# Loading half of x already transposed, and running two products of blocks two and three between the token halves of block one

## Chip, core and metric

The kernel runs on one core of one Trainium2 chip. The metric is the device time of one execution in microseconds (us). The engines are named as in the profile: PE is TensorE's matmul side and PEld its weight load, DVE is VectorE, ACT is ScalarE, POOL is GpSimd, SP is SyncE. SP issues nearly all transfers, in order.

## What is computed

One layer of an encoder trunk, cut to what matters here:

```python
h = rms_norm(x, norm_w)                       # x is 1024 tokens x 2048 columns, float32
proj = h @ w_in                               # 2048 x 6656: 13 column blocks of 512
y = concat(retention(rq, rk, rv) * silu(rg), window_attention(aq, ak, av) * silu(ag))
out = rms_norm(x + y @ w_out, final_norm_w)
```

The change touches only the start of `h @ w_in`. The norm weight `nw` belongs to a column of x and the factor `rms` to a token. Since `rms` multiplies whole tokens, the kernel may put it on the result of the projection instead of on x.

## The kernel before

**Products.** A float32 operand is split into a high part in the type float32r and the remainder, also float32r. A product of two split operands is three matmuls (`mm3`, lines 99, 100, 101: high times high, high times remainder, remainder times high). One matmul has a 128x128 weight and 512 columns. ACT makes the high part of a weight operand (`operand`, line 194), DVE the remainder (`low`, line 85). The weight operands have two buffers (`AHEAD`), so the next one can only be written when the product before last is done.

**Blocks.** The projection is worked off in column blocks of 512, each in two halves of the depth (`PHASES`). The first phase takes five blocks (`akv`, `aq0`, `aq1`, `rk0`, `rq0`) with the first 1024 columns of x; below they are blocks one to five. Blocks two and later use Winograd's form of Strassen's scheme: seven products instead of eight (numbers 1, 2, 6, 5, 7, 3, 4), whose operands are sums of quarters of w (`a11`, `a12`, `a21`, `a22`, made by DVE with `add`, line 92, and `sub`, line 95) and sums of quarters of x (tiles `c1` to `c7`, split on ACT, line 88, and DVE, line 85). Block one needs no sums of x, so it is computed plainly, with eight products.

**Steps.** A product is four steps of six matmuls; `advance()` counts a step, and generators (`start`, `tick`, `idle`) hang work on the count. Block one takes 32 steps, every later block 28. The order of PE, SP and POOL is as written. For the first 33 steps the order of DVE and ACT is as written as well (`all_manual`); after that a scheduler in the build places their instructions, moving them ahead of others where it sees a gap, except those that `behind()` pins.

**The opening.** x arrives with tokens on the partitions. Four 128x128 transposes on PE turn one column group of one token half into a bank `ax` (lines 1017, 1037 and 470), and ACT and DVE read it. For tokens 0 to 511 they write the high part (line 999), the remainder (line 1003) and a copy (lines 1009, 1011), all unscaled by `rms`. For tokens 512 to 1023 the rows are scaled by `rms` first, then turned. The sums of squares (`squares`, ACT line 448, DVE line 450) give `rms`; transposed into a row over tokens (`rows`), it scales the first half's copy (line 1089). The unscaled results of block one and of product 1+2 of block two go to memory, are loaded again later, multiplied by `rows` and stored again (lines 1102 to 1109). Matmuls of the identity with itself (line 1147) run on PE until the first data are there.

**After the sums.** Once the tiles of x are made, `keep` writes them to memory, and `second_part` loads the other 1024 columns of x transposed (`x_t`), scales them (line 509) and forms the sums for the second depth half, while blocks four and five run. A quarter of w is loaded by `quarter` (line 201) into the one buffer of its kind, as soon as the operand made from the old one is finished. The results leave the banks `pj` through ACT copies (`evict`, line 328) and DVE adds (line 92) into eight buffers `ct`, from which SP stores them (line 290).

Of the kernel before, what the change touches and what calls it, by code (L numbers as in the profile page):

```python
# [18 lines left out]
P = 128  # L19
SQ = 32  # L20
S = 1024
# [37 lines left out]
def hybrid_layer_kernel(  # L59
    ctx: ExitStack,  # L60
    tc: tile.TileContext,
    x, x_t, w_in, w_out, norm_w, decay_fwd, decay_bwd, gn_w, gn_b, sink, final_norm_w,
# [106 lines left out]
    rows_d = dram.tile([1, HALF], F32, name="rows_d")  # L169
# [37 lines left out]

    def operands():

        for u in range(len(units)):  # L210
            a = dict(w_next)
            if u == 0:

                for (n, k), last in zip(QUARTERS + QUARTERS[:2], (False, False, True, True, True, True)):
                    if (n, k) == (1, 1):
                        if not last:
                            left = wp.tile([P, M, 2 * P], F32R, name="s2", tag="s2")
                        op = wp.tile([P, M, 2 * P], F32R, name="wH", tag="wH", bufs=AHEAD), left
                        if last:
                            nc.scalar.copy(out=op[0], in_=a[n, k])  # L220
                        else:
                            split(*(t[:, 0:2] for t in op), a[n, k][:, 0:2])
                    else:
                        op = operand(a[n, k])
                    if last:
                        w_next[n, k] = quarter(*units[1], n, k)
                    yield op
                continue

            def then(n, k):  # L230
                if u + 1 < len(units):
                    w_next[n, k] = quarter(*units[u + 1], n, k)
                else:
                    place_free(n, k)

# [59 lines left out]
    def evict_second(b, i, a, bank, held):  # L295

        def store(n, m, t):
            stores.append((True, pr[BLOCKS[b] // P + 2 * n + a][:, half(m)], t))

        if i == 1:  # L300
            held["u", a] = t = ct()
            nc.scalar.copy(out=t, in_=bank)
            held[1, a] = ct()
            nc.vector.tensor_tensor(out=held[1, a], in0=t, in1=rows_of[0], op=ALU.mult)
        elif i in (6, 5):
            held[i, a] = ct()
            add(held[i, a], bank, held[1, a])
        else:
            t = held.pop(({2: "u", 7: 5, 3: 6, 4: 1}[i], a))
            add(t, bank, t)  # L310
            store(*{2: (0, 0), 7: (1, 1), 3: (0, 1), 4: (1, 0)}[i], t)
            if i == 2:
                unscaled.append(stores[-1][1])
# [25 lines left out]
    unscaled, rows_of = [], []  # L339

# [4 lines left out]
    def first_block(b, of):  # L345


        ops_, t = {}, 0
        for m, order in ((0, QUARTERS), (1, QUARTERS[2:] + QUARTERS[:2])):
            for n, k in order:  # L350
                if k == 1:
                    banks = [pj(), pj()]
                if t not in (0, 3, 4):
                    prepare()
                if t not in (4, 5):
                    ops_[n, k] = ready.popleft()
                wH, wL = ops_[n, k]
                for q in range(M):
                    if q == M - 1:
                        flush()  # L360
                    for a in range(2):
                        cH, cL = of[k, m]
                        if t == 0 and q < 2:
# [5 lines left out]
                            for po, w in left:  # L369
                                nc.tensor.matmul(po, w, cL[:, q], start=False, stop=False)  # L370
# [1239 lines left out]
```

## Time and profile before

| | us |
|---|---|
| median of 3 runs (lowest to highest) | 1515.04 (1514.44 to 1516.33) |
| the profiled execution: its own time | 1510.86 |
| the profiled execution: its span | 1508.7 |
| PE busy in the span | 1487.5 |
| DVE busy in the span | 1116.5 |
| ACT busy in the span | 681.2 |

The span is the time from the first to the last instruction; the execution's own time is 2.2 us longer. Mean durations of an instruction include a stretch in which the next one already runs, so work is best costed from the distance between starts. A group's row ends with the idle time before it and what ended that. In the table of windows a row gives for each engine the busy time and the count, then the granted clock, the share of the DMA engines and GB/s.

### The profile page before, as it was taken

Reading aid. Unit: us, or ns where it says so; the run is one execution under the profiler, and the core shown is the slowest. Engines: PE = TensorE matmul, PEld = TensorE weight load, DVE = VectorE, ACT = ScalarE, POOL = GpSimd, SP = SyncE. Lnnn points to the kernel's source line nnn. Section 1 sums busy time; section 2 is a strip of 40 time slices with the busy share of each in tenths; the row PEclk is TensorE's granted clock in tenths of the full one; section 3 lists DMA queues with packets and bytes.
Section 4 is the critical chain, followed back from the end, with each engine's and each line's share of the span. In section 5 each row is a group of like instructions: output and inputs, shape, how many; then the busy total and the mean of one; then the engine's idle time right before and its main releaser. Section 6 shows DMA issues by size and latency. Waiting matters only on the chain.

```text
span 1508.7 us, 20071 instructions
## 1 busy us (share of the span) xinstructions
PE 1487.5 (99%) x7154; PEld 1250.8 (83%) x7154; DVE 1116.5 (74%) x1928; ACT 681.2 (45%) x1108; POOL 150.9 (10%) x177
## 2 busy tenths in 40 slices
PE   9999999999999999999999999999999999999997
PEld 8878788888888888888888788887888888888886
DVE  6898694557768576767988789887656966776766
ACT  7533363334545454533444444444444664542425
POOL 0000001111010000011221100001211102020001
PEclk9999999999999999999999999999999999999999
DMA  8278748889584636798867665589887899495656
GB/s 329 63 281 346 286 168 215 226 202 259 143 265 154 196 133 199 287 311 196 175 160 170 161 193 170 183 290 335 218 235 190 180 211 207 96 207 169 213 178 254
DMA packets 140997, 318.88 MB, mean 211 GB/s; under 512 B 31425, under 2 KB 53345, under 8 KB 131554
## 3 DMA queue, kind: packets, MB, share of 16 engines
q1 hardware_dynamic: 116850, 266.74, 53.0%
q0 software_dynamic: 19728, 36.71, 16.5%
q10 hardware_dynamic: 4320, 14.17, 2.8%
q8 instruction: 56, 0.92, 0.3%
q14 instruction: 43, 0.35, 0.1%
HBM read 197.23 MB, written 128.71 MB: 216 GB/s over the span
## 4 chain that ended last, share of the span: by engine, by line
PE 83%; DVE 5%; issue 5%; DMA 4%; POOL 1%; ACT 1%; SPq 0%; POOLq 0%; ACTq 0%; DVEq 0%
PE pj L101 21%; PE pj L99 21%; PE pj L100 21%; PE ax L100 5%; PE ax L101 5%; PE ax L99 5%; PE ax L874 2%; DVE wL L85 2%; PE ax L656 1%; DMA pr<-ct 1%; DMA g<-mix 1%; PE ax L844 1%; PE ax L925 1%; POOL pr L292 1%; DMA ct<-pr 1%
## 5 line engine op out<-in xcount | busy, mean ns | idle before, releaser
L99 PE MATMUL pj<-c,wH 128*128 128x512 f32 x1444 | 573.1, 397 | 2.6 <-ACT wH L194 2.6
L101 PE MATMUL pj<-c,wL 128*128 128x512 f32 x1440 | 563.9, 392 | 6.6 <-DVE wL L85 6.5
L100 PE MATMUL pj<-c,wH 128*128 128x512 f32 x1444 | 563.6, 390 | 0.0
L101 PEld LDWEIGHTS pj<-c,wL 128*128 128x128 f32 x1440 | 270.8, 188 | 68.2 <-DVE wL L85 11.0
L99 PEld LDWEIGHTS pj<-c,wH 128*128 128x128 f32 x1444 | 271.9, 188 | 54.7 <-ACT wH L194 3.8
L100 PEld LDWEIGHTS pj<-c,wH 128*128 128x128 f32 x1444 | 272.0, 188 | 51.5 <-DVE c L1003 0.2
L85 DVE TENSOR_TENSOR wL<-a,wH 128x1024 fp32r<-128x1024 f32 x157 | 191.2, 1218 | 103.1 <-ACT wH L194 54.3
L194 ACT CAST wH<-a 128x1024 fp32r<-128x1024 f32 x129 | 135.5, 1050 | 176.7 <-PE pj L100 142.3
L328 ACT COPY ct<-pj 128x512 f32<-128x512 f32 x192 | 111.2, 585 | 209.3 <-PE pj L101 192.6
L92 DVE TENSOR_TENSOR ct<-pj,ct 128x512 f32<-128x512 f32 x164 | 108.7, 684 | 39.8 <-PE pj L101 39.4
L292 POOL DMA_DIRECT2D pr<-ct x88 | 78.0, 960 | 527.8 <-DVE ct L92 433.7
L85 DVE TENSOR_TENSOR wL<-s,wH 128x1024 fp32r<-128x1024 f32 x56 | 68.3, 1221 | 57.9 <-ACT wH L194 50.7
L100 PE MATMUL pj<-wL,c 128*128 128x512 f32 x224 | 87.2, 389 | 0.6 <-DVE wL L85 0.6
L99 PE MATMUL pj<-wH,c 128*128 128x512 f32 x224 | 87.1, 389 | 0.0
L101 PE MATMUL pj<-wH,c 128*128 128x512 f32 x224 | 87.1, 389 | 0.0
L100 PE MATMUL ax<-wL,c 128*128 128x512 f32 x208 | 81.2, 390 | 0.0
L99 PE MATMUL ax<-wH,c 128*128 128x512 f32 x208 | 80.9, 389 | 0.0
L101 PE MATMUL ax<-wH,c 128*128 128x512 f32 x208 | 80.9, 389 | 0.0
L88 ACT CAST wH<-a 128x1024 fp32r<-128x1024 f32 (+1 forms) x30 | 30.7, 1023 | 61.9 <-PE pj L101 35.0
L194 ACT CAST wH<-s 128x1024 fp32r<-128x1024 f32 x50 | 52.5, 1051 | 6.9 <-DVE s L95 6.9
L646 ACT ACTIVATE s<-s,nm 128x385 f32<-128x385 f32 (+1 forms) x64 | 37.6, 589 | 28.5 <-DVE nm L641 26.2
L100 PEld LDWEIGHTS pj<-wL,c 128*128 128x128 f32 x224 | 42.0, 188 | 9.8 <-DVE wL L85 1.0
(242 smaller groups left out, 2063.9 us busy)
## 6 DMA issues: line engine op xcount, KB each, us to landing
a<-in_w_in_dram SPq DMA_DIRECT2D x103, 512.0 KB, 5.3
kept<-c SPq DMA_DIRECT2D x28, 1024.0 KB, 7.7
c<-kept SPq DMA_DIRECT2D x28, 1024.0 KB, 7.4
pr<-ct SPq DMA_DIRECT2D x94, 256.0 KB, 5.5
pr<-ct POOLq DMA_DIRECT2D x88, 256.0 KB, 5.7
a<-in_w_out_dram SPq DMA_DIRECT2D x18, 512.0 KB, 4.5
rx<-pr SPq DMA_DIRECT2D x64, 128.0 KB, 5.7
ysrc<-pr ACTq DMA_DIRECT2D x16, 512.0 KB, 6.5
```

Of the source, the lines that this page charges most:

```text
L85: return nc.vector.tensor_tensor(out=dst, in0=src, in1=high.bitcast(F32), op=ALU.subtract)
L88: behind(pinned, nc.scalar.copy(out=dst_h, in_=src))
L92: nc.vector.tensor_tensor(out=dst, in0=a, in1=b, op=ALU.add)
L99: nc.tensor.matmul(po, aH, bH, start=first, stop=False, **kw)
L100: nc.tensor.matmul(po, aH, bL, start=False, stop=False, **kw)
L101: nc.tensor.matmul(po, aL, bH, start=False, stop=last, **kw)
L194: behind(pinned, nc.scalar.copy(out=wH, in_=src))
L292: nc.gpsimd.dma_start(out=dst, in_=t, accum_op=ALU.add)
L328: nc.scalar.copy(out=t, in_=bank)
L646: nc.scalar.activation(out=s[:, 0:w + 1], in_=s[:, 0:w + 1], func=AF.Exp, scale=-1.0, bias=nm, accum_out=den)
L656: nc.tensor.transpose(pt[:, blk(j)], s[:, blk(j)], ident)
L874: nc.tensor.matmul(p, k_tok[:, c // 2, :, c % 2], vd[:, c, d], start=True, stop=True)
```

## The change

**x transposed.** The first 1024 columns of x come a second time as input `x_f`, with columns on the partitions, cut into column half and token half; they are loaded straight into `src0`. The 64 transposes of x are gone, and with them the copies out of the banks. x with tokens on the partitions is still loaded, for the sums of squares alone. The norm weight and two other vectors come as one small input `vecs`.

**Order of PE.** Block one's first token half (16 steps) is followed by products 1 and 2 of blocks two and three (`early`, 8 steps each, unscaled, on the unscaled first token half), then by block one's second half (16 steps), then by the other five products of blocks two and three in the order 5, 6, 3, 7, 4 (`rest`). So the step at which block three ends, 88, is the same as before.

**Scaling.** DVE multiplies each column group by `nw` and `rows` at once (`scale`, line 1087). Product 1 of blocks two and three waits in its banks and is scaled into `ct` (line 414); the sum of products 1 and 2 is stored unscaled (8 tiles instead of 6) and rescaled later from `rows` directly (line 1228).

**Written order.** A table `plan` gives the work of ACT and DVE by step; their order is as written up to step 66 instead of 33. `second_part` starts at step 76 instead of 62.

The core of the diff:

```diff
+    def mixed(a, then):
+        a11, a12, a21, a22 = (a[q] for q in QUARTERS)
+        s2 = wp.tile([P, M, 2 * P], F32, name="s2", tag="s2")
+        sub(a11, a11, a21)
+        yield
+        add(a21, a21, a22)
+        yield
+        op = [wp.tile([P, M, 2 * P], F32R, name=n, tag=n, bufs=AHEAD) for n in ("wH", "wL")]
+        nc.scalar.copy(out=op[0], in_=a21)
+        yield
+        sub(s2, a22, a11)
+        yield
+        low(op[1], a21, op[0])
+        then(2, 1)
+        yield op
...
-            behind(clock[0] >= 33, sub(a11, a11, a21))
+            behind(True, sub(a11, a11, a21))
             sub(s2, a22, a11)
             yield op
-            yield operand(s2, clock[0] >= 33)
+            yield operand(s2, True)
...
+    def rest(b):
+        if b not in held_of:
+            first_scaled(b)
+        held = held_of[b]
+        Y, X = [pj(), pj()], [pj(), pj()]
+        for i in (5, 6, 3, 7, 4):
+            if b != units[1][1] or i == 4:
+                prepare()
+            bank = X if i in ON_X else Y
+            products(i, bank, ready.popleft(), comb[i], i in (5, 6), True, lambda a: evict_rest(b, i, a, bank[a], held))
...
+                if p == 0 and b in blocks[:3]:
+                    if b == blocks[0]:
+                        plain(b, 0, quarters, first_ops)
+                        for e in blocks[1:3]:
+                            early(e)
+                        plain(b, 1, quarters, first_ops)
+                    else:
+                        rest(b)
...
-        if clock[0] == 33:
+        if clock[0] == 66:
             all_manual.close()
...
+    load_first(0, 0, 0, 1)
+    nc.scalar.dma_start(out=vec_t, in_=vecs)
+    half_of_a11(0)
+    load_first(0, 0, 1, 1)
+    half_of_a11(2)
+    load_first(0, 0, 2, 2)
+    a12 = quarter(*u0, 1, 2)
+    load_first(1, 0, 0, 2)
+    load_first(1, 0, 2, 2)
+    a21 = quarter(*u0, 2, 1)
+    a22 = quarter(*u0, 2, 2)
...
+    idling = pj()
+    for _ in range(18):
+        nc.tensor.matmul(idling[:, 0:P], ident, ident, start=True, stop=True)
...
+    w_next[1, 1] = quarter(*u1, 1, 1)
+    load_row(4)
+    load_row(5)
+    w_next[1, 2] = quarter(*u1, 1, 2)
+    load_row(6)
+    load_row(7)
+    early_quarter(1)
+    load_row(0)
+    load_row(1)
+
+    def load_rest():
+        load_natural(6, 2, 3)
+        load_row(2)
+        early_quarter(2)
+        load_row(3)
+        load_first(0, 1)
...
+    at(22, square, 3, 0, True)
+    at(22, square, 3, 1, False)
+    at(23, factors_of, 0, 4)
+    at(24, lambda: ready.append(operand(early_w[2])))
...
+    at(76, lambda: start(second_part()))
```

Three places show the moved instructions. The first is the start of ACT's program, with the waits of each row. `vec_t` holds the norm weight, `c1` the split x, `a11` a quarter of w, `xt` and `src` are x before and after it is turned. Before:

```order
L526 DMA vec_189<-in_norm_w_dram 16x128
L436 DMA xt_183<-in_x_dram 128x2x256 x2
L1155 ACT_TABLE_LOAD
L1155 COPY vec_t_169<-pj_228 128x16 [waits PE_49]
L88 CAST wH_247<-a11_192 128x512 [waits DMAHW3_49]
L999 ACTIVATE c1_220<-ax_215,vec_t_169 128x512 [waits DVE_49,PE_49]
```

Now:

```order
L992 DMA vec_t_168<-in_vecs_dram 128x32
L989 DMA a11_190<-in_w_in_dram 128x512 x2
L1012 ACT_TABLE_LOAD [waits DMAHW1_49,DMAHW0_49]
L1012 ACTIVATE c1_207<-src_181,vec_t_168 128x512 [waits DVE_49]
L1012 ACTIVATE c1_207<-src_181,vec_t_168 128x512 [waits DMAHW3_49]
```

The table load had no wait; now it stands behind two transfers (the first piece of x and `vecs`).

The second place is DVE from the last operand of block two (`wL`, product 4) on. `wL` is the remainder of a weight operand, `ct` results, `a11`, `a21`, `s2` the sums of w, `c1`, `c2`, `c4` tiles of x. Before, down to the second operand of block three:

```order
L85 TENSOR_TENSOR wL_890<-a22_390,wH_889 128x1024
L85 TENSOR_TENSOR c1_220<-src_182,c1_220 128x1024 x2
L92 TENSOR_TENSOR ct_801<-pj_686,ct_801 128x512
L92 TENSOR_TENSOR ct_806<-pj_687,ct_806 128x512
L85 TENSOR_TENSOR wL_929<-a11_816,wH_928 128x1024
L85 TENSOR_TENSOR c2_221<-src_182,c2_221 128x1024 x2
L92 TENSOR_TENSOR ct_727<-pj_684,ct_727 128x512
L92 TENSOR_TENSOR ct_734<-pj_685,ct_734 128x512
L85 TENSOR_TENSOR wL_969<-a12_818,wH_968 128x1024
```

Now, down to the first operand that block three still needs (product 5):

```order
L85 TENSOR_TENSOR wL_866<-a22_373,wH_865 128x1024
L414 TENSOR_TENSOR ct_946<-ax_506,rows_270 128x512
L85 TENSOR_TENSOR c4_853<-tt_688,c4_853 128x1024
L92 TENSOR_TENSOR ct_779<-pj_750,ct_779 128x512
L92 TENSOR_TENSOR ct_784<-pj_751,ct_784 128x512
L95 TENSOR_TENSOR a11_829<-a11_829,a21_697 128x1024
L85 TENSOR_TENSOR c2_208<-src_181,c2_208 128x1024
L92 TENSOR_TENSOR a21_697<-a21_697,a22_869 128x1024
L95 TENSOR_TENSOR s2_902<-a22_869,a11_829 128x1024
L85 TENSOR_TENSOR c2_208<-src_181,c2_208 128x1024
L85 TENSOR_TENSOR wL_906<-a21_697,wH_905 128x1024
```

Block three used to begin with quarters of w as they are loaded; now its next product needs a sum, and nine instructions stand between the two operands where four stood.

The third place is DVE in block four, up to the operand of product 6 (`wL<-s2`). `src` is the second depth half of x, scaled in place by line 509 (now 537), `tt` its sums. Before:

```order
L85 TENSOR_TENSOR wL_1211<-a11_1090,wH_1210 128x1024
L509 SCALAR_TENSOR_TENSOR src_982<-src_982,vec_t_169,rows_522 128x1024 x2
L95 TENSOR_TENSOR tt_1339<-src_982 128x1024
L85 TENSOR_TENSOR wL_1252<-a12_1092,wH_1251 128x1024
L95 TENSOR_TENSOR a11_1090<-a11_1090,a21_1052 128x1024
L95 TENSOR_TENSOR tt_1340<-src_982,tt_1339 128x1024
L95 TENSOR_TENSOR s2_1255<-a22_1172,a11_1090 128x1024
L1108 TENSOR_TENSOR ct_1189<-ct_1189,ct_1187 128x512
L1108 TENSOR_TENSOR ct_1190<-ct_1190,ct_1187 128x512
L92 TENSOR_TENSOR a21_1052<-a21_1052,a22_1172 128x1024
L95 TENSOR_TENSOR tt_1388<-src_982 128x1024
L85 TENSOR_TENSOR wL_1296<-s2_1255,wH_1295 128x1024
```

Now (the operands of products 1 and 2 stand further up, with two more scalings, a sum and two adds behind the first of them):

```order
L95 TENSOR_TENSOR s2_1154<-a22_1072,a11_1038 128x1024
L537 SCALAR_TENSOR_TENSOR src_1032<-src_1032,vec_t_168,rows_270 128x1024
L92 TENSOR_TENSOR a21_910<-a21_910,a22_1072 128x1024
L537 SCALAR_TENSOR_TENSOR src_1032<-src_1032,vec_t_168,rows_270 128x1024
L95 TENSOR_TENSOR tt_1340<-src_1032,tt_1339 128x1024
L95 TENSOR_TENSOR tt_1386<-src_1032 128x1024
L537 SCALAR_TENSOR_TENSOR src_1032<-src_1032,vec_t_168,rows_270 128x1024 x2
L95 TENSOR_TENSOR src_1032<-src_1032 128x2x512
L95 TENSOR_TENSOR tt_1387<-src_1032,tt_1386 128x1024
L92 TENSOR_TENSOR ct_1182<-pj_1148,ct_1182 128x512
L92 TENSOR_TENSOR ct_1187<-pj_1149,ct_1187 128x512
L85 TENSOR_TENSOR wL_1191<-s2_1154,wH_1190 128x1024
```

Between the finished sum `s2` and the operand made from it there stood 4 instructions; now there are 11, eight of them scalings and sums of the second depth half.

More of the change, by code (lines that the diff above doesn't have):

```diff
@@ L293, in flush, with evict_rest @@
         stores.clear()
[L295 to L305, printed above, removed]
+    def evict_rest(b, i, a, bank, held):
+        if i in (5, 6):
             held[i, a] = ct()
@@ L502, in second_part @@
                 yield from idle(3)
-        rows = rows_of[1]
-        yield from rows_from(rms[:, 4:8], rows[:, half(1)])
         yield
@@ L1068, in rows_from @@
[L1068 to L1099 removed]
+    quarters, first_ops = {}, {}
@@ new lines, in hybrid_layer_kernel @@
+    load_row(5)
[11 more added lines that the diff above has]
+        load_first(0, 1)
+        for n in (2, 1), (2, 2):
+            w_next[n] = quarter(*u1, *n)
+        load_first(1, 1)
+    both = st.tile([P, S], F32, name="rows")
+    rows_of.extend((both[:, half(0)], both))
+    factors = {}
@@ new lines, in spread, with turn_rows, scale @@
+    def spread(m):
+        t = factors[m] = st.tile([P, HALF], F32, name="factors")
+        nc.vector.tensor_copy(out=chunks(t), in_=rms[:, 4 * m:4 * m + 4].rearrange("p (t o) -> p t o", o=1).broadcast_to([P, 4, P]))
+    def turn_rows(m, pt):
+        for t in range(4):
+            nc.tensor.transpose(pt[:, blk(t)], factors[m][:, blk(t)], ident)
+        nc.scalar.copy(out=both[:, half(m)], in_=pt)
+    def scale(s, k, m):
+        t, i = src0[:, s, k, half(m)], s * M + k
+        nc.vector.scalar_tensor_tensor(out=t, in0=t, scalar=nw[:, i:i + 1], in1=both[:, half(m)], op0=ALU.mult, op1=ALU.mult)
@@ new lines, in hybrid_layer_kernel, with step, at @@
+    mixed_first = mixed(w_next, then_of(1))
+    def step(n=1):
+        for _ in range(n):
+            if (op := next(mixed_first)) is not None:
+                ready.append(op)
+    plan = {}
+    def at(n, what, *args):
+        plan.setdefault(n, []).append((what, args))
+    at(6, lambda: ready.append(operand(w_next[1, 1])))
+    at(8, square, 4, 0, True)
+    at(8, square, 4, 1, True)
+    at(10, square, 5, 0, True)
+    at(10, square, 5, 1, False)
+    at(11, lambda: ready.append(operand(w_next[1, 2])))
@@ L1100, in scale_first, with opening, rescaled @@
+    at(76, lambda: start(second_part()))
+    at(112, lambda: start(decays()))
+    def opening():
+        for n in range(max(plan) + 1):
+            for what, args in plan.get(n, ()):
+                what(*args)
+            yield
+    def rescaled():
+        yield from idle(74)
         for i in range(0, len(unscaled), 2):
-            r = ct()
-            nc.sync.dma_start(out=r, in_=rows_d.to_broadcast([P, HALF]))
             es = [ct() for _ in range(2)]
```

501 lines of the change are left out of this document (237 added, 264 removed).

## The prediction

> **What bounds the kernel now.** I read the page's busy times first, then the windows of the opening, the waits of PE, and the timeline of DVE where PE waits. The page:
>
> ```profile
> span 1508.7 us, 20071 instructions
> PE 1487.5 (99%) x7154; PEld 1250.8 (83%) x7154; DVE 1116.5 (74%) x1928; ACT 681.2 (45%) x1108; POOL 150.9 (10%) x177
> ```
>
> PE is idle for 21 us of the whole span. So a change gains by taking work off PE or by closing a wait of PE, and nothing else. The change ends with block four; behind it the order hangs on PE's steps, so that a time won or lost there is carried to the end. The opening in windows (last column GB/s):
>
> ```profile
> 5.00:10.00 5.00, 4.78 (x27) 4.28 (x26) 2.31 (x4) 2.06 (x4) 0.00 (x0) 1.00 1.05 377
> 10.00:15.00 5.00, 5.00 (x32) 4.30 (x31) 3.72 (x6) 4.09 (x7) 0.00 (x0) 1.00 1.03 419
> 15.00:20.00 5.00, 5.00 (x28) 4.04 (x27) 4.82 (x7) 4.79 (x8) 0.00 (x0) 1.00 1.02 419
> 20.00:25.00 5.00, 5.00 (x23) 4.00 (x22) 4.67 (x9) 4.83 (x9) 1.24 (x1) 1.00 0.97 397
> 60.00:80.00 20.00, 19.64 (x87) 15.93 (x86) 19.90 (x21) 9.94 (x12) 0.00 (x0) 1.00 0.26 79
> 80.00:100.00 20.00, 19.29 (x85) 15.37 (x83) 20.00 (x22) 10.28 (x11) 0.00 (x0) 1.00 0.64 217
> ```
>
> Up to 25 us the DMA engines are full, and between 60 and 100 us DVE is: 39.9 of 40 us. There PE already waits for DVE's remainders of weight operands (first 160 us; columns: total, times, longest):
>
> ```profile
> PE pj L101 <- DVE wL L85: 1.1, 2, 0.7
> ```
>
> So this stage has two limits that lie close together, PE and DVE. DVE's pace there, back to back:
>
> ```profile
> 62.13 1.22 DVE L85 TENSOR_TENSOR wL<-a,wH 128x1024 fp32r<-128x1024 f32 x1
> 63.27 1.22 DVE L95 TENSOR_TENSOR a<-a,a 128x1024 f32<-128x1024 f32 x1
> ...
> 67.81 1.28 DVE L304 TENSOR_TENSOR ct<-ct,rows 128x512 f32<-128x512 f32 x2
> 69.02 1.22 DVE L92 TENSOR_TENSOR a<-a,a 128x1024 f32<-128x1024 f32 x1
> ...
> 124.95 2.48 DVE L509 SCALAR_TENSOR_TENSOR src<-src,vec_t,rows 128x1024 f32<-128x1024 f32 x2
> 127.34 1.28 DVE L92 TENSOR_TENSOR ct<-pj,ct 128x512 f32<-128x512 f32 x2
> ```
>
> From start to start, 1024 elements cost 1.14 us, 512 cost 0.60 (two in 1.21), and the two-factor scaling costs 1.195 (two in 2.39). For 512 elements I estimate that scaling at 0.66: the fall from 1.14 to 0.60 taken from 1.195. PE's pace shows where ACT waits for products:
>
> ```profile
> 127.19 1.06 ACT L194 CAST wH<-a 128x1024 fp32r<-128x1024 f32 x1 [3.66 <-PE pj L100]
> 132.62 1.05 ACT L194 CAST wH<-a 128x1024 fp32r<-128x1024 f32 x1 [4.38 <-PE pj L100]
> ```
>
> A product is 5.43 us, a step 1.3575. ACT's cast can only start when the product that used its buffer ends, so these two are the ends of the fifth and the sixth of block three's seven products, and block three ends at 132.62 + 5.43 = 138.05.
>
> **The start: nothing.**
>
> ```profile
> 1.36 2.93 PE L1147 MATMUL pj<-ident 128*128 128x128 f32 x12 [1.36 <-POOL ident masks.py:199]
> ...
> 2.25 1.28 ACT L1155 ACT_TABLE_LOAD   x1 [2.25 <-issue]
> ...
> 5.27 0.62 ACT L88 CAST wH<-a 128x512 fp32r<-128x512 f32 x1 [0.56 <-DMA a<-in_w_in_dram]
> ...
> 7.57 0.61 PE L1147 MATMUL pj<-ident 128*128 128x128 f32 x4
> ...
> 8.40 0.50 PE L366 MATMUL pj<-c,wH 128*128 128x512 f32 x1 [0.22 <-ACT c L999]
> ```
>
> The first real matmul starts at 8.40. Six identity matmuls are 12 records of 0.244 us; the last two are four records of 0.15. The 18 of the changed kernel are 36 records without a gap: they end at 1.36 + 8.8 = 10.2 if all go at the first pace and at 1.36 + 2.93 + 24 x 0.15 = 7.9 if all but 12 go at the last. I take 8.5. ACT's chain is behind that cover: the table load now waits for the first piece of x and the vector, about 5.3 by the piece of w that landed at 5.27, plus 1.28 for the load and about 0.6 for a pass over 512 columns: 7.2.
>
> **The transposes: -6.2 us of PE.** Of the 64, eight lie before 8.40. The other 56 stand between matmuls; in the chain that ended last each group of four costs
>
> ```profile
> 12.32 0.44 PE ax L1037 x4
> ```
>
> so 14 x 0.44 = 6.2. The two groups that turn the rows stay. Counted from 8.5, 88 steps and 0.9 for those two end at 128.9, against 138.05: 9.2 less, 6.2 of it transposes and the rest the waits and slips of the old opening. This is what PE would gain if nothing made it wait.
>
> **Input and the start of DVE's long stretch: 43.8 us.** Now x comes twice.
>
> ```profile
> 25.55 1.06 ACT L448 ACTIVATE junk<-xt 128x1024 bf16<-128x1024 f32 x1 [0.40 <-DMA xt<-in_x_dram]
> ```
>
> Here ACT waits for the last row tile of the old first list, 8.4 MB behind the start (2.1 of x, four quarters of 0.52, four rows of 1.05). In the new list SP queues 14.7 MB up to row tile 3, the last that the first token half's `rms` needs: 2.1 of x, eight quarters of w and eight row tiles. The 6.3 MB more take 15.0 us at 419 GB/s, so it lands at about 40.5. On ACT follow a square (1.06), two bank copies and the cast of block three's second operand.
>
> ```profile
> L194 ACT CAST wH<-a 128x1024 fp32r<-128x1024 f32 x129 | 135.5, 1050 | 176.7 <-PE pj L100 142.3
> L328 ACT COPY ct<-pj 128x512 f32<-128x512 f32 x192 | 111.2, 585 | 209.3 <-PE pj L101 192.6
> ```
>
> That is 1.06 + 2 x 0.585 + 1.05 = 3.3, so DVE gets to that operand's remainder at 43.8. PE needs it at step 28, 8.5 + 38.0 + 0.4 = 46.9: in time. The Trainium skill ("DMA: Bandwidth & Descriptors", Bandwidth) puts what HBM gives one core at about 358 GB/s; by it the 6.3 MB take 17.6 us and everything below comes 2.6 later. The windows show 397 to 419, so the measurement decides.
>
> **Blocks two and three: PE waits 6 us.** From 43.8 on DVE always has the next instruction ready. Up to the last operand of block two (`wL_866`) the order has 27 of 1024 elements, 16 scalings, 19 of 512 and a spread of the factors, which no quoted row shows and which I put at 0.4, below an operation of 512: 30.8 + 10.6 + 11.4 + 0.4 = 53.2. I add 1.4 for two places where DVE must wait, once for ACT's cast of a sum made one instruction earlier (1.05) and once for a product. It ends at 98.3. PE without waits begins that product (step 64) at 96.3 and needs the remainder 0.45 later, behind two matmuls of 0.226: 1.5 us of wait. Up to `wL_906`, the operand of block three's first remaining product, come 7 more of 1024 and 3 of 512, 9.8 us: 108.2. In there the quarter `a22` also has to land; its buffer is free at 98.3, and
>
> ```profile
> a<-in_w_in_dram SPq DMA_DIRECT2D x103, 512.0 KB, 5.3
> ```
>
> makes it 103.6, just as DVE reaches its sum. PE would need `wL_906` at 96.3 + 1.5 + 5.43 + 0.45 = 103.7: another 4.5 us. From there 26.7 us of matmuls lead to the end of block three at 134.9, 3.1 us before 138.05. So of the 9.2, 6.0 are waited away. The cause is the order: product 5 comes first and needs a sum of two quarters, one of which is loaded only when the block before is finished with the old one.
>
> **Block four: PE waits 6.7 us more.** I count from the end of block three's last product but one, 134.9 - 5.43 = 129.5. DVE adds its results (1.2), makes the operand of block four's product 1 (1.1) and then, up to `wL_1191`, has 10 of 1024, 6 scalings of 1.195 and 4 of 512: 11.4 + 7.2 + 2.4 = 21.0. With 0.1 of handing over it is 152.9. PE needs it after product 4, eight steps and 0.45: 134.9 + 11.3 = 146.2. The same sum for the old kernel, from the adds on, is 15.0 (9 of 1024, 2 scalings, 4 of 512), and the trace confirms it:
>
> ```profile
> 133.26 1.28 DVE L92 TENSOR_TENSOR ct<-pj,ct 128x512 f32<-128x512 f32 x2
> ...
> 147.18 1.22 DVE L85 TENSOR_TENSOR wL<-s,wH 128x1024 fp32r<-128x1024 f32 x1
> 148.31 1.22 DVE L95 TENSOR_TENSOR tt<-src,tt 128x1024 f32<-128x1024 f32 x1
> ```
>
> 133.26 to 148.3 is 15.0, and PE's need was at 138.05 + 11.3 = 149.35, one us later. So the old kernel had no wait here. The new one is at 152.9: 3.6 us behind it.
>
> **Behind that: zero, -1 to +2.4.** In the old block four DVE, in order, stood 5.7 us in front of a rescaling whose load was late, and operands behind it were late:
>
> ```profile
> 162.42 1.29 DVE L1108 TENSOR_TENSOR ct<-ct 128x512 f32<-128x512 f32 x2 [5.73 <-DMA ct<-pr]
> 165.36 1.22 DVE L85 TENSOR_TENSOR wL<-s,wH 128x1024 fp32r<-128x1024 f32 x1 [1.64 <-ACT wH L194]
> ```
>
> SP had issued that load at 153.21, 9.2 us ahead:
>
> ```profile
> 153.21 2.76 SPq L1105 DMA_DIRECT2D ct<-pr  x2
> ```
>
> The operand was due at 138.05 + 27.15 + 0.45 = 165.65; its high part came at 165.36 and its remainder at 166.5, which with the third matmul pushed back cost about 1. In the new order SP stands, ahead of the load, in front of a quarter of w whose buffer is free only when product 7's operand is made: product 6 ends at 157.9, then a copy, a cast and a remainder, 160.7. With the load 1 us behind that and 5.3 to 9.2 us long, a rescaling (0.6) and the remainder (1.1), product 3's operand is there at 168.7 to 172.6; it is due at 152.9 + 16.3 = 169.2. So the wait is 0 to 3.4 where about 1 was. I take no difference. Small vectors, `decays` without its transpose and the dropped broadcast load run beside full PE and count nothing; uncovered they are under 0.5.
>
> **Sum.** -9.2 + 6.0 + 6.7 = +3.5; from the two instants, 152.9 - 149.35 = +3.6. The profiled execution took 1510.86, so 1514.5; on the median of 1515.04 it is 1518.6. A measurement of this kernel can tell about 0.2%, 3 us, from no change.
>
> **Rivals.**
> - *DVE keeps up (faster).* All 9.2 remain and the time is 1505.8. It decides at `wL_906`: PE without waits needs it at 96.3 + 5.43 + 0.45 = 102.2, so DVE's 64.4 us from 43.8 on would have to be 6.0 shorter, or start so much earlier, and in block four another 6.7 would have to fall into gaps. For it: DVE has little to do before 40 us. Against: what it lacks there is the data, and the same way of adding met the old trace within 0.1 us. Chance 0.16.
> - *Only one of the two waits.* Without the first, block three ends at 128.9 and the second is counted from 123.5: 146.9, which is 2.5 ahead of 149.35, 1512.5. Without the second the 3.1 remain: 1511.9. For it: the two have different causes. Against: none of the rows says which would go. Chance 0.20.
> - *Transfers late (slower still).* At the 377 of the 5 to 10 us window the 6.3 MB take 16.7 instead of 15.0, and with the upper end in block four the sum is 1.7 + 2.4 more: 1522.7. For it: SP's one queue carries 4 MB more in the first 45 us, and the second token half and the stores follow on it. Against: 419 held for 10 us. Chance 0.16. At the 358 of the skill's page the shift alone is 2.6, 1521.2, a time inside this rival.
> - *It does not do what it says.* The transposes are gone from PE's order, but the start is not earlier; that is in the sum already.
>
> **Numbers.** The forecast has 0.48. Of it I count 0.10 within 0.2%, its sum being so near the limit. Faster by over 0.2%: 0.16 and 0.05 of the second rival, 0.21. Within: 0.10 + 0.15 = 0.25. Slower: 0.38 + 0.16 = 0.54. Cases of both signs hold the chance; the forecast's own range is 1516 (DVE's waits of 1.4 gone and the load of block four on time) to 1522 (a start at 10.2 instead of 8.5, which puts the adds of product 2 and with them 43.8 back by 0.6, and that load late). The range to hold 8 in 10 leaves out the first rival and the top of the last: 1511 to 1524.
>
> **What would show it.** L368 starts at 8 to 9 us and no transpose of x stands between its matmuls; the windows DVE full from 44 to 108 us and again from 121 to 152; the waits of PE a row for `wL` of line 85 of 11 to 13 us in the first 160, with two waits over 4 us, on block three's product 5 and block four's product 6. The prediction is wrong if PE has no idle time there, or if DVE has gaps before the remainder of `a21` plus `a22`; and its size is wrong if row tile 3 lands far from 40.5.

## The result, and the profile after

The changed kernel takes 1519.93 us (median of 13 runs), the kernel before 1512.99 (13 runs): a ratio of 1.0041, interval 1.0028 to 1.0054, so 4 to 8 us slower. One of the 13 executions took 6239 us and is left out of the ratio; the median of the other 12 is 1519.4. The profiled execution took 1520.48, its span is 1518.7, against 1510.86 and 1508.7.

The page after: the span has grown by 10.0 us, PE's busy time has shrunk by 1.4. So PE stands still for 11.4 us more than before.

```profile
span 1518.7 us, 19938 instructions
PE 1486.1 (98%) x7100; PEld 1249.5 (82%) x7100; DVE 1118.0 (74%) x1932; ACT 671.1 (44%) x1090; POOL 149.0 (10%) x176
```

Where was it lost? One and the same short wait of PE, for an operand of the second phase, in the timeline of PE before and after:

```profile
271.11 0.50 PE L101 MATMUL pj<-c,wL 128*128 128x512 f32 x1 [0.41 <-DVE wL L85]
```

```profile
278.58 0.50 PE L101 MATMUL pj<-c,wL 128*128 128x512 f32 x1 [0.91 <-DVE wL L85]
```

It is 7.5 us later, so the whole loss lies in the first 280 us. (At 1041 us the distance is still 6.9; the other 3 us of this pair of executions come at 1242 us and are looked at in the last section.) The waits of PE from 20 to 270 us, before and then after (total, times, longest):

```profile
PE pj L101 <- DVE wL L85: 1.6, 3, 0.7
```

```profile
PE pj L101 <- DVE wL L85: 6.2, 1, 6.2
PE pj L99 <- DVE ct L92: 5.9, 2, 5.4
```

There are two long waits, as forecast, but the first is not for an operand `wL`. It is for an addition into a result buffer `ct`. The timeline of DVE there:

```profile
95.64 1.28 DVE L92 TENSOR_TENSOR ct<-pj,ct 128x512 f32<-128x512 f32 x2
96.84 1.22 DVE L95 TENSOR_TENSOR tt<-src,tt 128x1024 f32<-128x1024 f32 x1
97.98 1.22 DVE L85 TENSOR_TENSOR wL<-a,wH 128x1024 fp32r<-128x1024 f32 x1
99.11 0.69 DVE L414 TENSOR_TENSOR ct<-ax,rows 128x512 f32<-128x512 f32 x1
99.71 1.22 DVE L85 TENSOR_TENSOR c<-tt,c 128x1024 fp32r<-128x1024 f32 x1
100.84 1.28 DVE L92 TENSOR_TENSOR ct<-pj,ct 128x512 f32<-128x512 f32 x2
```

`wL_866` is the row at 97.98 and is there at 99.2. PE restarts only at 101.68, after the first of the two additions at 100.84. They read the banks of product 7, and product 4 goes on adding in these very banks (`ON_X` holds 6, 7 and 4, and `rest` runs 5, 6, 3, 7, 4), so it can't start before they are read. What PE does then, in the timeline of PE:

```profile
95.84 0.39 PE L101 MATMUL pj<-c,wL 128*128 128x512 f32 x1
101.68 0.76 PE L99 MATMUL pj<-c,wH 128*128 128x512 f32 x1 [5.45 <-DVE ct L92]
...
105.65 0.41 PE L99 MATMUL pj<-c,wH 128*128 128x512 f32 x1
...
148.10 0.39 PE L100 MATMUL pj<-c,wH 128*128 128x512 f32 x1
154.65 0.79 PE L101 MATMUL pj<-c,wL 128*128 128x512 f32 x1 [6.16 <-DVE wL L85]
...
160.32 0.39 PE L99 MATMUL pj<-c,wH 128*128 128x512 f32 x1
```

Nine matmuls start between 101.68 and 105.65, 0.44 us apart; elsewhere it is 0.226. The windows show why: the figure behind the five engines is the granted clock.

```profile
95.40:98.80 3.40, 0.83 (x4) 0.37 (x2) 3.40 (x5) 1.62 (x2) 0.00 (x0) 1.00 0.00 0
98.80:102.20 3.40, 0.52 (x1) 0.50 (x2) 3.40 (x6) 0.34 (x1) 0.00 (x0) 0.50 0.57 93
102.20:105.60 3.40, 3.40 (x9) 2.63 (x8) 3.40 (x4) 0.00 (x0) 0.00 (x0) 0.50 1.00 414
105.60:109.00 3.40, 3.40 (x16) 2.79 (x15) 3.40 (x4) 1.05 (x1) 0.00 (x0) 0.99 0.29 110
```

While PE waits, its clock falls to a half, and it stays there for 6.8 us: 9 matmuls in 3.4 us instead of 16. The nine from 101.68 to 105.65 take 4.0 us instead of 2.0, the thirteen from 154.65 to 160.32 take 5.7 instead of 2.9. So the two waits cost 1.9 and 2.7 us beyond their own length.

The account to 271 and 278 us: transposes -6.2; the start -0.5 (first real matmul at 7.92 instead of 8.40); waits 6.2 + 5.9 + 0.9 instead of 1.6 + 0.4, +11.0; low clock +4.6. That is +8.9; measured is +7.5, and the difference of 1.4 fits the old opening's small slips: up to 100 us the old kernel's matmuls lose about 3 us beyond 0.226 each, the new one's 0.7, and only a part of that is in the 6.2 of the transposes.

### The profile page after: what moved, and what is told of

It reads as the page before. It is cut to its first block, busy times and chain, and to the rows that moved or that the text cites. A ratio compares the mean times of both kernels' runs of the same rounds, so it can differ in the third digit from the quotient of the medians.

```text
span 1518.7 us, 19938 instructions
## 1 busy us (share of the span) xinstructions
PE 1486.1 (98%) x7100; PEld 1249.5 (82%) x7100; DVE 1118.0 (74%) x1932; ACT 671.1 (44%) x1090; POOL 149.0 (10%) x176
## 4 chain that ended last, share of the span: by engine, by line
PE 83%; DMA 6%; DVE 6%; issue 2%; ACT 1%; POOL 0%; SPq 0%; ACTq 0%; POOLq 0%; DVEq 0%
PE pj L101 21%; PE pj L99 21%; PE pj L100 21%; PE ax L100 5%; PE ax L101 5%; PE ax L99 5%; DMA xt<-in_x_dram 2%; PE ax L870 2%; PE ax L657 1%; DVE wL L85 1%; DMA pr<-ct 1%; DMA c<-kept 1%; PE ax L840 1%; DVE c L85 1%; DVE ct L92 1%
## 5 line engine op out<-in xcount | busy, mean ns | idle before, releaser
L99 PE MATMUL pj<-c,wH 128*128 128x512 f32 x1384 | 551.1, 398 | 8.5 <-DVE ct L92 5.9
L101 PE MATMUL pj<-c,wL 128*128 128x512 f32 x1384 | 544.1, 393 | 11.2 <-DVE wL L85 11.2
L100 PE MATMUL pj<-c,wH 128*128 128x512 f32 x1384 | 542.2, 392 | 0.0
L101 PEld LDWEIGHTS pj<-c,wL 128*128 128x128 f32 x1384 | 261.4, 189 | 71.1 <-DVE wL L85 15.6
L99 PEld LDWEIGHTS pj<-c,wH 128*128 128x128 f32 x1384 | 261.9, 189 | 58.9 <-issue 6.7
L100 PEld LDWEIGHTS pj<-c,wH 128*128 128x128 f32 x1384 | 261.9, 189 | 49.7
L85 DVE TENSOR_TENSOR wL<-a,wH 128x1024 fp32r<-128x1024 f32 x151 | 184.0, 1219 | 111.3 <-ACT wH L193 62.0
L193 ACT CAST wH<-a 128x1024 fp32r<-128x1024 f32 x121 | 127.1, 1050 | 168.2 <-PE pj L100 144.4
L335 ACT COPY ct<-pj 128x512 f32<-128x512 f32 x184 | 106.7, 585 | 202.0 <-PE pj L101 197.0
L92 DVE TENSOR_TENSOR ct<-pj,ct 128x512 f32<-128x512 f32 x170 | 112.7, 685 | 40.9 <-PE pj L101 40.4
L88 ACT CAST wH<-a 128x1024 fp32r<-128x1024 f32 x28 | 29.5, 1054 | 61.4 <-PE pj L101 35.0
L99 PEld LDWEIGHTS pj<-wH,c 128*128 128x128 f32 x224 | 42.5, 190 | 10.1 <-ACT wH L88 1.4
```

The costliest lines, as they stand in the source:

```text
L85: return nc.vector.tensor_tensor(out=dst, in0=src, in1=high.bitcast(F32), op=ALU.subtract)
L88: behind(pinned, nc.scalar.copy(out=dst_h, in_=src))
L92: nc.vector.tensor_tensor(out=dst, in0=a, in1=b, op=ALU.add)
L99: nc.tensor.matmul(po, aH, bH, start=first, stop=False, **kw)
L100: nc.tensor.matmul(po, aH, bL, start=False, stop=False, **kw)
L101: nc.tensor.matmul(po, aL, bH, start=False, stop=last, **kw)
```

## The experiments

All ratios are to the kernel before on the same chip (the changed kernel: 1.0041). Waits are those of PE in the one profiled execution.

**1. Two operand copies later (e1).** Copies `c1` and `c2`, written at steps 68 to 74, had been moved ahead; two of four stood in front of the first wait.

```diff
-        split(*(comb[i][:, hl, 2 * j:2 * j + 2] for hl in range(2)), of)
+        split(*(comb[i][:, hl, 2 * j:2 * j + 2] for hl in range(2)), of, i in (1, 2))
```

> Edit: the operand copies of products 1 and 2 for the second token half (c1, c2) stay where they are written, behind the remainder of a21 + a22 of block three; two of the four stood in front of block two's last product. Theory A (VectorE's written order sets both waits of TensorE): VectorE reaches the last additions ahead of block two's last product 2.3 us sooner, so the wait of 5.45 us there falls to about 3; block three's first remaining product still finds its operand; the wait of 6.2 us in block four stays between 5 and 7. Time 2 to 3 us under the changed kernel. Theory B (the input, which comes twice, is late, and the order only decides who shows it): the wait of 5.45 stays within 1 us and the time too.

Measured: 1.0045 (1.0028 to 1.0063), no change that can be told. The first wait fell only from 5.45 to 4.25, though DVE had 2.3 us less to do. (The wait in block four fell to 4.36, below the 5 to 7 expected; 0.84 came up behind it.) In its timeline DVE now stands idle itself, for a product of PE:

```profile
78.82 1.37 DVE L92 TENSOR_TENSOR ct<-pj,ct 128x512 f32<-128x512 f32 x2 [0.82 <-PE pj L101]
```

So the wait is not set by all of DVE's work since 44 us. From this addition, which hangs on PE's step 52, to the additions of product 7 DVE's order takes 20.4 us (78.82 to 99.21, of which 1.3 are waits for casts of ACT), and PE gets from step 52 to step 64 in 16.3.

**2. The second depth half later (e2).** Its eight scalings are pinned too.

```diff
-    at(76, lambda: start(second_part()))
+    at(84, lambda: start(second_part()))
...
-                nc.vector.scalar_tensor_tensor(out=src[:, s, k], in0=src[:, s, k], scalar=nw[:, i:i + 1], in1=rows_of[1], op0=ALU.mult, op1=ALU.mult)
+                behind(True, nc.vector.scalar_tensor_tensor(out=src[:, s, k], in0=src[:, s, k], scalar=nw[:, i:i + 1], in1=rows_of[1], op0=ALU.mult, op1=ALU.mult))
```

> Edit: the job that loads and scales the other half of x's columns starts at step 84 instead of 76, and its eight scalings are not moved ahead of what is written before them. Theory A: of the 21 us of VectorE work ahead of the operand of block four's product 6, some 12 go behind it; the wait of 6.2 us there and the low clock after it (2.4 us) go, the wait of 5.45 in block two stays. Time 6 to 8.6 us under the changed kernel, depending on what is late next (a rescaling's load, up to 2.4). Theory B: the wait stays, since the quarter of w that this operand needs lands late; time within 1.5 us of the changed kernel.

Measured: 1.0021 (1.0010 to 1.0031), 3 of the 6 us that the change had cost. The wait of 6.16 is 0.84, but product 3 of block four now waits:

```profile
149.09 0.50 PE L101 MATMUL pj<-c,wL 128*128 128x512 f32 x1 [0.84 <-DVE wL L85]
168.42 0.80 PE L101 MATMUL pj<-c,wL 128*128 128x512 f32 x1 [2.72 <-DVE wL L85]
```

Theory A is right on the place and the cause. Theory B (the quarter of w lands late) falls, and not by this run alone, which moves the loads of the second half too. In the changed kernel itself DVE makes the sum `s2` from that quarter early and then works without a gap until the operand:

```profile
140.45 1.23 DVE L95 TENSOR_TENSOR s<-a,a 128x1024 f32<-128x1024 f32 x1
...
153.37 1.22 DVE L85 TENSOR_TENSOR wL<-s,wH 128x1024 fp32r<-128x1024 f32 x1
```

The gain is half of what was expected: 2.72 us of wait come back, with a low clock behind them. The first wait is 4.25 here too, although DVE's order up to it is that of the changed kernel. In this execution row tile 3 had landed at 40.63 instead of 41.63 and PE had begun at 8.32 instead of 7.92. So executions differ by about 1.2 us in this wait, and e1's fall to 4.25 can't be put down to the moved copies.

**3. Both (e3).** 

> Both edits together. Theory A: the gains add, 2.5 + 7.5 = 10 us under the changed kernel, so about 3 us under the kernel before; of TensorE's waits of the first 160 us the one in block two is left with about 3. If they don't add, block four was late because block two and three were, and the time is that of the second edit alone. Theory B: as the changed kernel.

Measured: 1.0009 (0.9997 to 1.0022), level with the kernel before, 5 us under the changed one. That is half of the 10 us expected, and more than the single edits bring on their own (nothing that can be told, and 3 us). Waits of 7.7 us are left (4.25, 0.20, 0.57, 2.72). With waits like these the low clock can be seen alone, for the wait of 2.72 is the same in e2 and e3. The windows around it, e2 and then e3:

```profile
165.00:168.00 3.00, 0.70 (x4) 0.24 (x2) 3.00 (x4) 1.05 (x1) 0.00 (x0) 0.99 0.87 363
168.00:172.00 4.00, 3.58 (x10) 2.87 (x11) 4.00 (x6) 0.00 (x0) 0.00 (x0) 0.58 0.26 33
```

```profile
163.00:166.00 3.00, 0.70 (x4) 0.24 (x2) 3.00 (x4) 1.05 (x1) 0.00 (x0) 1.00 0.82 332
166.00:170.00 4.00, 3.58 (x16) 2.97 (x17) 4.00 (x6) 0.00 (x0) 0.00 (x0) 1.00 0.20 56
```

PE is idle for the same time in both; in e2 the clock falls and 10 matmuls run in the next 4 us, in e3 it does not and 16 run: 6 x 0.226 = 1.4 us. The last section shows what decides it.

**4. The waits filled (e4).** Identity matmuls ahead of the two products, so that PE is late but not idle.

```diff
+    held_of, fill = {}, lambda n: (lambda e: [nc.tensor.matmul(e[:, 0:P], ident, ident, start=True, stop=True) for _ in range(n)])(ax())
...
+            (b, i) == (units[1][1], 4) and fill(15)
...
+                    (p, b, i) == (0, blocks[3], 6) and fill(18)
```

> Edit: identity matmuls ahead of block two's last product (15) and of block four's product 6 (18), on a free bank; nothing else is to be earlier. Theory C (the long idle time itself lowers the granted clock, and the lower clock costs 1.75 and 2.45 us after the two waits): with about 4.5 and 5.4 us of the waits filled the granted clock stays at 1.00 through both, and the time is about 4 us under the changed kernel, though VectorE is as late as there. If the lower clock has another cause, or costs nothing since VectorE is the bound behind it as well, the time stays within 1 us of the changed kernel, or is above it by what the fillers delay.

Measured: 1.0031 (1.0018 to 1.0045); the intervals overlap, so no time gained can be claimed. But the first clock did stay up:

```profile
99.00:102.00 3.00, 1.72 (x13) 1.43 (x12) 3.00 (x5) 0.00 (x0) 0.00 (x0) 1.00 0.67 135
102.00:106.00 4.00, 4.00 (x19) 3.33 (x18) 4.00 (x4) 0.83 (x1) 0.00 (x0) 1.00 1.00 408
```

So idle time is what lowers it. The way from the restart of product 4 to the end of block three's product 7 took 28.97 - 0.79 - 0.42 = 27.8 us without its waits, against 29.75 - 0.43 = 29.3 in the changed kernel (both from restart to restart). The 1.5 us were given back: 0.79 at block three's product 5 and 1.44 in block four, where PE now came sooner than DVE. Behind the second wait 2.12 us of idle time were left, and the clock fell there all the same.

**5. Product 7 copied by ScalarE (e5, e6, e7).** ACT copies the banks of product 7 in blocks two and three, DVE adds from the copy; alone (e5), with both edits of e3 (e6), and with the second half started at step 80 as well (e7).

```diff
+            t = held.pop(({7: 5, 3: 6, 4: 1}[i], a)); e = ct() if i == 7 else bank
+            add(t, e, t) if i != 7 else (nc.scalar.copy(out=e, in_=bank), add(t, e, t))
```

> Edit: in blocks two and three ScalarE copies the banks of product 7, and VectorE adds from the copy; all else as in the changed kernel. Products 7 and 4 stand next to each other on the same banks, so TensorE cannot begin product 4 before product 7's result is read. Theory D (TensorE waits for that read, which stands in VectorE's order behind the operand, and not for the operand): the wait on an addition at about 101 us goes; in its place stands a wait for the remainder of a22, which ends at 99 to 100, so 2.5 to 3.5 us instead of 5.45; the later and shorter wait of 0.43 on product 4 of block three goes too. Theory A in its first form (the operand is the last to come): the wait stays within 1 us. In both the wait of about 6 us in block four stays: time 1.5 to 4 us under the changed kernel by D, the same by A.

> The two edits of the order and the copy of product 7's banks together. Theory D: the wait of 4.25 us that was left in block two with both edits of the order falls to about 1, and with it goes the low clock behind it; 4 to 5 us under the kernel with both edits, about 1509.5, 0.25% under the kernel before. If VectorE's amount of work in front of the operand sets the wait and not the read, 3 to 4 us of wait are left and the time is within 1.5 us of the kernel with both edits.

> As the three edits together, with the second half's job started at step 80 instead of 84. With both edits of the order TensorE waited 2.7 us in block four for the remainder made at 165 us, behind an addition and a scaling in VectorE's order, while VectorE stood idle 4.4 us ahead of block four's product 6. If these scalings fill that idle time, the 2.7 fall below 1 and the time is 2 us under the three edits. If the load of the rescaling or the addition set the 2.7, or if the scaling makes product 6 late again, it is the same or 1 to 2 us above.

Measured: 1.0057 (1.0036 to 1.0078), 1.0058 (1.0039 to 1.0077) and 1.0056 (1.0035 to 1.0077). None is below the changed kernel, where less was expected (the intervals overlap with its own), and e6 is 7 us above e3. The first wait did fall, to 3.77, 2.20 and 2.20. But block three paid; the wait in e5's PE, and ACT's row that ends it:

```profile
139.86 0.80 PE L99 MATMUL pj<-c,wH 128*128 128x512 f32 x1 [9.82 <-ACT ct L318]
```

```profile
139.22 1.07 ACT L318 COPY ct<-pj 128x512 f32<-128x512 f32 x2 [8.33 <-DMA pr<-ct]
```

The copy needs two of the eight `ct`, and the row puts ACT's wait down to a store of one of them. In e6 and e7 the same wait is 5.2 and 7.3.

**6. The copy in block two alone (e8, e9).** With e3's edits; `c4`'s second half is written behind the copy, so that ACT makes the copy first. e9 starts the second half at step 80.

```diff
+            t = held.pop(({7: 5, 3: 6, 4: 1}[i], a)); e = ct() if (b, i) == (units[1][1], 7) else bank
...
-    at(61, put, 4, 1)
+    at(64, put, 4, 1)
```

> The two edits of the order, and ScalarE's copy of product 7's banks in block two alone (in block three the copy stood waiting for one of the eight result buffers), with the second half of c4's operand written behind that copy. Theory D (TensorE waits for the read of product 7's banks): the wait of 4.25 us falls to 1 to 1.5 and leaves no low clock behind it; block three keeps its wait of 0.2. The time is 3 to 4 us under the kernel with both edits, about 1511. If the copy's two extra buffers make a later transfer late, as in block three, the gain is given back there and the time is that of both edits or above.

> As the one before it, with the second half's job started at step 80 instead of 84. If the scalings behind the addition set the wait of 2.7 us in block four, it falls below 2 and the time is about 1 us less; if the addition or the rescaling's load sets it, there is no difference.

Measured: 1.0025 (1.0014 to 1.0035) and 1.0026 (1.0013 to 1.0038). The first wait is 1.04, now for the operand, so Theory D holds: the read of product 7's banks had set it. The time is not the expected one, 1511, but that of its last sentence: the gain is given back. PE in e8:

```profile
97.80 0.50 PE L101 MATMUL pj<-c,wL 128*128 128x512 f32 x1 [1.04 <-DVE wL L85]
104.60 0.50 PE L99 MATMUL pj<-c,wH 128*128 128x512 f32 x1 [1.52 <-ACT wH L216]
106.34 0.50 PE L101 MATMUL pj<-c,wL 128*128 128x512 f32 x1 [1.01 <-DVE wL L85]
...
147.78 0.50 PE L101 MATMUL pj<-c,wL 128*128 128x512 f32 x1 [2.57 <-DVE wL L85]
167.13 0.80 PE L101 MATMUL pj<-c,wL 128*128 128x512 f32 x1 [2.71 <-DVE wL L85]
```

Of the 3.2 us won, 2.5 come back at block three's product 5 (the forecast's second wait, on `a21` plus `a22`), and 2.0 more at block four's product 6, which in e3 waited 0.57. e9's last wait is 2.17 instead of 2.71, which buys nothing in the time.

**7. Half of x with tokens on the partitions left out (e10).** The changed kernel without the loads and squares of row tiles 0 to 3. It takes the factors of the first 512 tokens from the sums of squares of the others, so it does not compute the layer and serves for its time alone.

> Left out: the loads and the squares of row tiles 0 to 3 (4.2 MB, 10 us of transfers); the first token half takes the norm of the second. All else as in the changed kernel. Theory B (the second copy of the input makes VectorE's long stretch begin late, and the waits follow from that): VectorE begins it several us sooner and the waits of 5.45 and 6.2 us shrink by as much, together by over 6 us. Theory D (between two results of TensorE, from about 79 to 101 us, VectorE has more work than TensorE gives it time): the first wait falls by 1.2 us at most, since VectorE then stands idle at 79 us for TensorE's product, as it did when two copies were moved; the second stays. Time 1 to 2 us under the changed kernel.

Measured: 1.0038 (1.0024 to 1.0053), as the changed kernel. The waits are 4.25 and 6.15, and DVE stands idle at 79 us for a product of PE. With 4.2 MB taken out of the first 45 us the first wait is no shorter than in e2, whose input is whole, and the second has not moved at all. Theory B falls here too: DVE gets to block three's second early operand 2.6 us sooner (42.16 instead of 44.73), but it waits for products of PE, 2.69 us at 40.70 and 0.57 at 79.18, so that the time is not used.

**8. Operands ahead of what waits (e11, e12).** In e3 the two waits of block four have one form. DVE's timeline in e3:

```profile
145.21 0.69 DVE L1228 TENSOR_TENSOR ct<-ct,rows 128x512 f32<-128x512 f32 x1 [4.37 <-DMA ct<-pr]
145.82 1.22 DVE L85 TENSOR_TENSOR wL<-s,wH 128x1024 fp32r<-128x1024 f32 x1
...
162.66 1.37 DVE L92 TENSOR_TENSOR ct<-pj,ct 128x512 f32<-128x512 f32 x2 [3.31 <-issue]
163.95 1.27 DVE L537 SCALAR_TENSOR_TENSOR src<-src,vec_t,rows 128x1024 f32<-128x1024 f32 x1
165.15 1.22 DVE L85 TENSOR_TENSOR wL<-s,wH 128x1024 fp32r<-128x1024 f32 x1
```

DVE is idle 4.4 us in front of an instruction that waits for a load, and 3.3 in front of an addition, and the operand that PE needs next stands behind it. (The second row names nothing that ended the wait. The addition starts at 162.66, and the last matmul of its bank, at 162.18, ends at 162.57 in PE's timeline, so it is read as a wait for PE.) The edit, on top of e3, keeps additions and rescalings behind the operands; e12 has e8's copy as well.

```diff
+            behind(i in (2, 7) and b == units[3][1], nc.vector.tensor_tensor(out=t, in0=bank, in1=t, op=ALU.add))
...
-            yield from idle(7)
+            yield from idle(9)
...
+                behind(True, nc.vector.tensor_tensor(out=e, in0=e, in1=rows_of[0], op=ALU.mult))
...
-            yield from idle(7)
+            yield from idle(5)
```

> The two edits of the order, and in block four VectorE's additions of products 2 and 7 and the rescalings stay behind the operand of the next product, which is written ahead of them (the rescalings two steps later). Theory: with both edits the waits left in block four (0.57 and 2.72 us) were operands that stood in VectorE's order behind an addition that waits for TensorE, or behind a rescaling whose load was late; with the operands ahead both waits go. Time about 3 us under the kernel with both edits, 1511, between 0.1 and 0.2% under the kernel before. If VectorE's amount of work or a transfer sets these waits, they come back at the next operand and the time is within 1 us of the kernel with both edits.

> The same, with ScalarE's copy of product 7's banks in block two. That copy had taken 3.2 us off the first wait, of which 2.5 came back in block three and 2 in block four. Theory: what came back in block four was the operand behind the late load; with it ahead the gain of block two stays, and the time is 1 to 2 us under the one before, 1509.5 to 1510. If each gain upstream is taken back by the next late operand, it is the same or above.

Measured: e11 0.9989 (0.9978 to 1.0000), 1510.18 us; e12 0.9981 (0.9969 to 0.9993), 1509.51 against 1511.90 for the kernel before on that chip. Both waits of block four are gone. PE's waits from 20 to 270 us in e11, and then in e12:

```profile
PE pj L99 <- DVE ct L92: 4.5, 2, 4.3
PE pj L101 <- DVE wL L85: 0.9, 1, 0.9
```

```profile
PE pj L101 <- DVE wL L85: 3.2, 4, 1.0
PE pj L99 <- ACT wH L216: 1.8, 1, 1.8
PE pj L99 <- DVE ct L92: 0.2, 1, 0.2
```

e12 is faster than both kernels, by 0.2% against the one before. Its distance to e11 is within the uncertainty; that the copy in block two adds something once block four is free is not shown.

## Why the prediction was right, and which of its steps were not

The side was right, and the size within the range: 1518.6 was forecast, +0.24%, a little under the interval of what was measured, +0.41% (0.28 to 0.54). The two waits were forecast at 6.0 and 6.7 us and measured at 5.9 and 6.2, but the first met its size by luck, from another cause, and the sum lacked a term, the low clock. Without that term's 4.6 us the loss of 7.5 us in the first 280 would be 2.9, near the 3.6 of the sum. By its own steps:

- **The start: nothing.** Right: 7.92 against 8.40. The 36 identity records took 6.8 us.
- **The transposes, -6.2, and 128.9 without waits.** Right. Product 4 of block two (step 64) was forecast to begin at 96.3 without waits; the matmul before it ends at 95.84 + 0.23.
- **Row tile 3 at 40.5, DVE's long stretch at 43.8.** Nearly. ACT's last square starts when the tile has landed, and the operand's cast follows two copies later, 0.9 late:

```profile
41.63 1.06 ACT L496 ACTIVATE junk<-xt 128x1024 bf16<-128x1024 f32 x1 [1.46 <-DMA xt<-in_x_dram]
```

- **Blocks two and three: 6 us, as 1.5 at product 4 and 4.5 at product 5.** The size of the sum was near, by luck; the place and the cause were not right. The step that failed is that PE needs nothing but the operand there, which "ends at 98.3": `wL_866` came at 99.2, but PE waited on to 101.68 for the additions of product 7. The forecast counted operands and left out that products 7 and 4 share their banks. e8 shows it: with the banks copied, PE waits 1.04 for `wL_866`, about the 1.5 of the forecast, and 2.5 at product 5. In the changed kernel the wait of 4.5 did not come: `wL_906` was there at 108.9 (forecast 108.2), and PE asked for it only at 109.53.
- **"A product is 5.43 us", behind a wait too.** Wrong, and this is the term that was missing. Product 4 of block two took 7.4 us, from 101.68 to 109.08, because its first nine matmuls ran at the low clock. That added 1.9 us here, and it added 2.7 behind the wait of block four. The 26.7 us from product 5's third matmul to the end of block three held. The windows of the kernel before show the low clock, behind a wait of 2.63 us that ends at 842.7:

```profile
844.00:848.00 4.00, 3.84 (x9) 3.10 (x10) 4.00 (x6) 1.97 (x3) 0.00 (x0) 0.50 0.35 95
```

  The forecast did not read it. The Trainium skill ("TensorE: Matmul & The Clock Gate", Part 1) says that the clock halves after an idle window of about 3.4 us and that the windows run free of the kernel. The 6.8 us of half clock (twice 3.4) and the pair e2 and e3 agree with free windows; that a wait of 2.72 us halved the clock in e2 does not agree with a whole idle window, and the measurement decides.
- **Block four: 6.7 us more, `wL_1191` at 152.9.** Right in mechanism and place, the wait was 6.16. Operand and need both came about 2 us later than forecast (154.6 and 148.3), because block three ended later. e2 shows the cause: with the scalings behind it the operand is in time.
- **Behind that: zero.** Near: the wait that the old kernel had there (0.52; the forecast put it at about 1) is gone. It was close, though: the operand came at 173.6, above the bounds of 168.7 to 172.6, and PE asked for it at 173.73 instead of 169.2, since all before it was later. In e2, e3 and e8, where PE came earlier, it was 2.7, within the bounds of 0 to 3.4, but an addition stood in front, not the load.
- **What would show it.** DVE was full where forecast, 62.65 of the 64 us from 44 to 108 and 29.78 of the 31 from 121 to 152. The row for `wL` is 6.2 instead of 11 to 13 us, and of the two places only block four's is right; this sign showed the miss in block two.
- **The rivals.** "DVE keeps up" and "only one of the two waits" didn't occur. "Transfers late" gave a time near the measured one, and for the wrong reason: e10 takes the transfers away and nothing is won. That DVE's row from 20 to 40 us shows so little work (10 instructions, 28 before) is real, but not the limit:

```profile
20.00:40.00 20.00, 20.00 (x91) 16.55 (x91) 6.36 (x10) 14.53 (x25) 1.03 (x1) 1.00 1.01 415
```

So the 6.2 us of transposes were saved on PE and lost, with interest, at two places of DVE's order. What is settled: the second wait is the scalings' (e2 and the changed kernel's own trace), the first the banks' read (e8), the clock follows the idle time (e4 and the last section), the input is not the limit (e10). What stays open is whether e8 (1.0025) is slower than e3 (1.0009) at all: their intervals overlap, e8's waits up to 170 us are 1.3 longer in sum, and the spans of the two profiled executions differ by 0.1.

## What to carry to other kernels

Work taken off the busiest engine is only worth something if the engine that feeds it is ahead of it; so cost the feeder's order between two points where it hangs on the busy engine, not over its whole stretch. In an in-order engine put the operand that is needed next ahead of every instruction that waits (an addition of a result, a rescaling behind a load), and where two products in a row add in the same banks, have the bank read at once (e8) or put another product between them (not run). A wait of PE has a second price, the half clock behind it: up to 2.7 us here. In this kernel it came for certain when PE stood still for 1.9 us or more of one window of 3.41 us (the last section), so by that count a wait of 3.8 us always pays it, since one window then holds at least half of it, and a shorter one pays it or not by where it falls (2.20 us did in e6 and did not in e7).

## What the runs showed of the hardware

The half clock comes on a grid. In all 14 profiles the stretches of half clock between 20 and 1490 us last 3.41, 6.83 or 10.24 us, and within one execution their starts lie whole multiples of 3.41 us apart, over more than 1100 us. What decides is how long PE stands still within one window of this grid. Of the windows at full clock, all 36 in which PE was idle for 1.9 us or more were followed by a window at half clock, and none of the 3665 in which it was idle for less than 1.57; in between it was 5 of 7. That explains the pair of e2 and e3. The wait of 2.72 us put 2.23 us of idle time into one window of e2; in e3 the grid cut it into 1.42 and 1.30. The windows of the grid, e2 and then e3:

```profile
164.52:167.93 3.41, 1.18 (x6) 0.64 (x4) 3.27 (x4) 1.05 (x1) 0.00 (x0) 1.00 0.93 372
```

```profile
161.71:165.12 3.41, 1.99 (x9) 1.31 (x7) 2.46 (x3) 1.05 (x1) 0.00 (x0) 1.00 1.00 377
165.12:168.54 3.42, 2.12 (x9) 1.78 (x10) 3.42 (x4) 0.00 (x0) 0.00 (x0) 1.00 0.22 93
```

Several short waits add up within a window. In the changed kernel at 1239 to 1242 us two waits of 0.95 and 0.76 us were enough; the windows there:

```profile
1238.90:1242.30 3.40, 1.70 (x6) 1.05 (x6) 1.23 (x1) 1.06 (x2) 0.00 (x0) 1.00 1.09 184
1242.30:1245.70 3.40, 3.40 (x9) 2.63 (x8) 0.00 (x0) 0.70 (x1) 0.00 (x0) 0.50 0.97 261
```

PE was busy for 1.70 of 3.40 us, and the next window ran at half clock; the kernel before had one wait of 0.58 there and kept its clock. Seven of the 13 profiles with the changed start have a window of half clock there, so the 3 us are not in every execution. In e12 a wait of 1.80 us within one window was enough (the half clock begins at 105.81). So executions of one kernel may differ by 1.4 to 2.7 us for each wait of this size; the runs of each kernel spread by 3.5 to 10 us. The executions of the changed kernel fit that in the main: three with a mean granted clock of 0.991 took 1521.5 to 1522.7 us, four with 0.993 took 1516.0 to 1518.3 (the profiled one, with 0.990, took 1520.5). That the place on the grid is the reason was not tried, since each kernel has one profile.

The 36 identity records of the start, which wait for nothing, took 5.78 to 7.21 us in the profiled executions of the changed kernel and the experiments, though the granted clock reads 1.00 there. Why is open.
